# Prompt attention in a decoder layer: transposes and scores in one gap between weight tiles, scaling and softmax in the other

## The chip, the cores and the metric

The kernel runs on one core of one Trainium2 chip. The metric is device time in microseconds (us), the median of the runs shown. The engines are called as the profile calls them: PE (TensorE matmuls), PEld (its weight loads), DVE (VectorE), ACT (ScalarE), POOL (GpSimd) and SP (SyncE).

## The reference, cut to what matters

One layer of a hybrid decoder runs on a prompt of 256 rows and on 8 samples of 8 rows that share the weights. One input projection gives the columns of a short gated convolution (B, C, h), of attention (q, k, v) and of two gates. The change concerns only the prompt's attention: 16 query heads and 4 key heads of width 64, in blocks of 128 queries over at most 256 keys.

```
def window_attend(q, k, v, dist, valid, rel_bias, sinks):
    s = einsum(q, k) * HEAD_DIM ** -0.5
    s = where(valid, s + bias, -inf)
    m = maximum(max(s), sink)
    p = exp(s - m)
    p = p / (sum(p) + exp(sink - m))
    return einsum(p, v)
```

The rest of the layer is matrix products: the projections, two output projections, their gated sum through `w_o`, and a SwiGLU of width 5632.

## The kernel before, in words

All products go through `product`. Weights arrive in tiles of 4 x 128 rows by 256 columns (`wraw`, 4 buffers, loaded on SP's queue). ACT rounds each tile to a high part (`whi`, L129) and DVE takes the remainder (`wlo`, L130), three buffers each. PE then does 24 matmuls for a tile (L186): high by high, high by low, low by high, for 4 row chunks and 2 column blocks, each streaming 320 columns of activations. The first use of `wlo` is the ninth matmul of its tile.

Attention is side work. It is a Python generator, and `tick()` advances it by one `yield` after each weight tile of the products for q, C, H and B. What the generator emits between two yields therefore stands between two weight tiles in PE's order; a scheduler may move single instructions by a few places, and the order on each engine is then fixed. One gap between two weight tiles is called a gap here, and the work emitted into it a slot.

The prompt's attention has 8 units (a key head and a pair of query heads). For each unit i the functions are:

- `bias_load`: a DMA on POOL's queue that fetches the unit's bias (2 buffers, `bias`).
- `prompt_scores`: six score matmuls (L541 into `ps1`, L544 into `ps0`), then four DVE operations (L549 to L553) that add the bias and fold two parts into the tile `s` (3 buffers).
- `prompt_softmax`: a maximum on DVE (L561), two small DVE operations (L562, L566), four exponentials on ACT (L569) and a small one (L572).
- `prompt_norm`: denominator and reciprocal (L576, L577) and four scalings of `s` on DVE (L579).
- `prompt_pt`: four PE transposes of `s` (L585, into `pp`), a copy on ACT (L586) and two masked copies on DVE (L588) into `pT` (4 buffers).
- `prompt_pv`: for each pair of units, 12 products with v (L601, into `po`); both halves of `po` leave through ACT (L611, high part) and DVE (L612, low part). It runs for units 0 to 3 in step 6 and for units 4 to 7 in step 10.

`pp`, `ps1`, `ps0` and `po` all come from one ring of 4 PSUM buffers (`ps_aux`); a new one waits until the buffer's last content, four allocations earlier, has been read by DVE and ACT.

In step i the kernel before puts into one slot the scaling of unit i-2 (emitted at the end of the step ahead) and the scores of unit i; into the next slot the softmax of unit i, then any products with v, then the transposes of unit i-2.

Two places outside attention matter as well. After the prompt's attention come the samples' (L658 to L726), which puts a few more small groups of matmuls between weight tiles until about 221 us. From there on PE runs weight tile after weight tile; the next foreign matmuls are a sum over partitions (L207) at 715 us and a single short matmul of the function `nudge` (L914) at 729 us.

Of the kernel before, what the change touches and what calls it, by code (L numbers as in the profile page):

```python
# [52 lines left out]
def hybrid_layer(ctx: ExitStack, tc: tile.TileContext, a: dict, o: list):  # L53
# [18 lines left out]
    def ps_aux(name):  # L72
        return aux[0].tile([P, 512], F32, tag="aux", name=name)
# [3 lines left out]
    def u(s):  # L77
        uid[0] += 1
        return f"{s}_{uid[0]}"
# [129 lines left out]
    def flip(ap):  # L209

        *rest, (step, n) = ap.ap
        return bass.AP(ap.tensor, ap.offset + (n - 1) * step, [*rest, (-step, n)])
# [270 lines left out]
    def q2(ch, par):  # L483
        o = LEAD_A + ch * at_row + par * TP
        return at_t[:, o:o + TP]
# [34 lines left out]
    def bias_load(kv, gp):  # L520
        bias = pr.tile([P, 2, 2 * WIN], F32, tag="bias", name=u("bias"), bufs=2)
        nc.gpsimd.dma_start(
            bias,
            bass.AP(
                e_scr.tensor, e_scr.offset + (kv * GRP + gp * 2) * EL, [[1, P], [EL, 2], [1, 2 * WIN]]
            ),
        )
        return bias

    def prompt_scores(kv, gp, bias):  # L530

        j, par = kv // 2, kv % 2
        s = pr.tile([P, 4, WIN], F32, tag="s", name=u("s"), bufs=3)
        ps1, ps0 = ps_aux(u("ps1")), ps_aux(u("ps0"))
        for gi in range(2):
            q = q2(j * 4 + gp * 2 + gi, par)
            for i in range(2):  # L540
                nc.tensor.matmul(  # L541
                    ps1[:, gi * 256:(gi + 1) * 256], q[:, WIN:2 * WIN], k2[:, kv, i], start=i == 0, stop=i == 1
                )
            nc.tensor.matmul(  # L544
                ps0[:, gi * 256:(gi + 1) * 256].rearrange("p (two k) -> p two k", two=2), q[:, 0:WIN],
                k2[:, kv, :, 0:WIN], start=True, stop=True,
            )
        w = pr.tile([P, 2, 2 * WIN], F32, tag="w", name=u("w"), bufs=1)
        nc.vector.tensor_add(w, ps1.rearrange("p (g k) -> p g k", g=2), flip(bias))  # L549
        nc.vector.tensor_max(s[:, 2:4], w[:, :, 0:WIN], w[:, :, WIN:2 * WIN])  # L550
        p0 = ps0.rearrange("p (g two k) -> p g two k", g=2, two=2)
        nc.vector.tensor_add(s[:, 0:2], p0[:, :, 0], flip(bias[:, :, 0:WIN]))
        nc.vector.tensor_add(s[:, 0:2], p0[:, :, 1], s[:, 0:2])  # L553
        return s

    def prompt_softmax(kv, gp, s):
        h0 = kv * GRP + gp * 2
        mx = wk.tile([P, 2, 2], F32, tag="mx", name=u("mx"))
        den = wk.tile([P, 2, 2], F32, tag="den", name=u("den"))
        es = wk.tile([P, 2, 2], F32, tag="es", name=u("es"))  # L560
        nc.vector.tensor_reduce(mx.rearrange("p b g -> p (b g)"), s, axis=AX.X, op=ALU.max)  # L561
        nc.vector.scalar_tensor_tensor(  # L562
            mx, mx, -1.0, nsink[:, h0:h0 + 2].unsqueeze(1).to_broadcast([P, 2, 2]),
            op0=ALU.mult, op1=ALU.min,
        )
        nc.vector.tensor_add(es, sink_bc[:, h0:h0 + 2].unsqueeze(1).to_broadcast([P, 2, 2]), mx)  # L566
        for n in range(4):
            b, g = n // 2, n % 2
            nc.scalar.activation(  # L569
                s[:, n], s[:, n], AF.Exp, bias=mx[:, b, g:g + 1], accum_out=den[:, b, g:g + 1]  # L570
            )
        nc.scalar.activation(es, es, AF.Exp)  # L572
        return den, es

    def prompt_norm(s, den, es):
        nc.vector.tensor_add(den, den, es)  # L576
        nc.vector.reciprocal(den, den)  # L577
        for n in range(4):
            nc.vector.tensor_scalar(s[:, n], s[:, n], den[:, n // 2, n % 2:n % 2 + 1], None, op0=ALU.mult)  # L579

    def prompt_pt(s):
        pt = pr.tile([P, 3, 2 * WIN], F32, tag="pT", name=u("pT"), bufs=4)
        pp = ps_aux(u("pp"))
        for n in range(4):
            nc.tensor.transpose(pp[:, n * WIN:(n + 1) * WIN], s[:, n], ident)  # L585
        nc.scalar.activation(pt[:, 0, :], pp[:, 0:256], AF.Copy)  # L586
        for b in range(2):
            nc.vector.tensor_mul(  # L588
                pt[:, 1 + b, :].rearrange("p (g q) -> p g q", g=2),
                pp[:, 256:512].rearrange("p (g q) -> p g q", g=2),  # L590
                sides[:, b:b + 1].to_broadcast([P, 2, WIN]),
            )
        return pt

    def prompt_pv(j, gp, pts):
        po = ps_aux(u("po"))
        steps = ((0, 0, 0, True, True), (1, 0, 1, True, False), (1, 1, 2, False, True))
        for b, t, kb, st_, sp_ in steps:
            for par in range(2):
                kv = j * 2 + par  # L600
                nc.tensor.matmul(  # L601
                    po[par * 64:(par + 1) * 64, b * 256:(b + 1) * 256],
                    vn[t][:, kv * HD:(kv + 1) * HD], pts[par][:, kb, :], start=st_, stop=sp_,
                )
        for g in range(2):
            src = po.rearrange("p (b g s j) -> p g b s j", b=2, g=2, j=JS)[:, g]
            ch = j * 4 + gp * 2 + g
            two_to(*(x(ch)[:, 0:TP // JS, :].rearrange("p (b s) j -> p b s j", b=2) for x in (at_h, at_l)), src)
# [5 lines left out]
    def prompt_attention():  # L614
        units = [(j * 2 + par, gp) for j in range(2) for gp in range(2) for par in range(2)]
        bias, sc, sm, pts = {}, {}, {}, {}
        bias[0] = bias_load(*units[0])
        for i in range(len(units) + 3):
            if i < len(units):
                if i + 1 < len(units):  # L620
                    bias[i + 1] = bias_load(*units[i + 1])
                sc[i] = prompt_scores(*units[i], bias.pop(i))
                yield
                sm[i] = prompt_softmax(*units[i], sc[i])
            if i >= 3 and (i - 3) % 4 == 3:
                for n in (i - 5, i - 3):
                    kv, gp = units[n]
                    prompt_pv(kv // 2, gp, (pts.pop(n - 1), pts.pop(n)))
            if 0 <= i - 2 < len(units):
                pts[i - 2] = prompt_pt(sc.pop(i - 2))  # L630
            yield
            if 0 <= i - 1 < len(units):
                prompt_norm(sc[i - 1], *sm.pop(i - 1))
            if i >= len(units):
                yield

    W2 = WIN + TS

# [117 lines left out]
    def attention():  # L756
        yield from prompt_attention()
        pr_p.close()
        with tc.tile_pool(name="sm", bufs=1, side="right") as sm:
            yield from sample_attention(sm)  # L760
# [505 lines left out]
```

## Time and profile before

| what | value |
|---|---|
| median of 3 runs | 1601.17 us (1601.07 to 1602.27) |
| the profiled execution: its own time, its span | 1601.14 us, 1599.4 us |
| busy: PE, DVE, ACT | 1590.5, 885.7, 651.4 us |
| the prompt's attention (first score matmul to last product with v) | about 91 to 174 us |
| DVE busy from 120 to 140 us | 19.89 of 20 us |

The profile's span runs from the first to the last instruction; the time of the run is 1.7 us longer. The times of matmuls in the trace overlap: one matmul of 320 columns is shown with 302 ns, but the next one starts 140 ns later. So what a matmul costs PE is read from the distance of starts, or from the chain of work that ended last, whose pieces do not overlap.

### The profile page before, as it was taken

The numbers are of one execution on the slowest core, as the hardware profiler recorded it, in microseconds if no ns is written. First come the engines' busy times: TensorE is split into PE (matmuls) and PEld (weight loads), VectorE is DVE, ScalarE is ACT, GpSimd is POOL, SyncE is SP. The second block draws the span as 40 slices with busy tenths as digits, with TensorE's granted clock in tenths as the row PEclk, the third lists the DMA queues.
The fourth block names the chain that finished last, engine by engine and source line by source line (L and its number), as shares of the span: only waits on it lengthen the run. The fifth ranks groups of instructions, "written<-read, shape, count | busy, mean of one in ns | idle before, by whom it ended". The sixth has DMA issues, their size and how long they took to land.

```text
span 1599.4 us, 26405 instructions
## 1 busy us (share of the span) xinstructions
PE 1590.5 (99%) x10955; PEld 1555.2 (97%) x10955; DVE 885.7 (55%) x1315; ACT 651.4 (41%) x928; POOL 78.3 (5%) x123
## 2 busy tenths in 40 slices
PE   9999999999999999999999999999999999999998
PEld 9999999999999999999999999998888999999887
DVE  7879565445555555556555555553444455555556
ACT  7555433433333334444333333333333334444443
POOL 1101311000000003320000000000000000000000
PEclk9999999999999999999999999999999999999999
DMA  8554546545454544544444455455555544545552
GB/s 276 174 168 138 184 146 195 169 156 156 156 157 157 159 158 158 157 156 152 157 158 159 158 158 158 157 153 163 155 156 157 156 157 158 159 158 157 185 173 93
DMA packets 74399, 258.13 MB, mean 161 GB/s; under 512 B 8552, under 2 KB 11928, under 8 KB 74152
## 3 DMA queue, kind: packets, MB, share of 16 engines
q1 hardware_dynamic: 71880, 249.86, 49.6%
q0 software_dynamic: 1968, 5.90, 1.3%
q8 instruction: 86, 1.41, 0.4%
q10 hardware_dynamic: 432, 0.69, 0.1%
q14 instruction: 33, 0.27, 0.0%
HBM read 253.30 MB, written 5.08 MB: 162 GB/s over the span
## 4 chain that ended last, share of the span: by engine, by line
PE 99%; DVE 0%; ACT 0%; issue 0%; DVEq 0%
PE fu L186 19%; PE fg L186 18%; PE dn L962 9%; PE ga L186 7%; PE wo L186 7%; PE gc L186 7%; PE dn L970 6%; PE B L186 3%; PE C L186 3%; PE H L186 3%; PE ya L186 3%; PE yc L186 3%; PE q L186 3%; PE dl L966 2%; PE kv L366 2%; PE dn L1116 1%
## 5 line engine op out<-in xcount | busy, mean ns | idle before, releaser
L130 DVE TENSOR_TENSOR wlo<-wraw,whi 128x1024 fp32r<-128x1024 f32 (+1 forms) x461 | 562.5, 1220 | 584.7 <-ACT whi L129 473.2
L129 ACT ACTIVATE whi<-wraw 128x1024 fp32r<-128x1024 f32 (+1 forms) x461 | 485.8, 1055 | 713.0 <-PE fu L186 129.5
L186 PE MATMUL fu<-hl_t,whi 128*128 128x320 f32 x704 | 205.3, 302 | 0.0
L186 PE MATMUL fu<-hh_t,whi 128*128 128x320 f32 x704 | 205.3, 302 | 0.0
L186 PE MATMUL fg<-hh_t,whi 128*128 128x320 f32 x704 | 205.2, 302 | 0.0
L186 PE MATMUL fg<-hl_t,whi 128*128 128x320 f32 x704 | 205.2, 302 | 0.0
L186 PE MATMUL fu<-hh_t,wlo 128*128 128x320 f32 x704 | 159.0, 302 | 0.0
L186 PE MATMUL fg<-hh_t,wlo 128*128 128x320 f32 x704 | 158.9, 301 | 0.0
L962 PE MATMUL dn<-a_t,whi 128*128 128x512 f32 x640 | 157.9, 383 | 0.0
L186 PEld LDWEIGHTS fu<-hh_t,whi 128*128 128x128 f32 x704 | 131.9, 187 | 0.0
L186 PEld LDWEIGHTS fg<-hh_t,whi 128*128 128x128 f32 x704 | 131.8, 187 | 0.0
L186 PEld LDWEIGHTS fg<-hl_t,whi 128*128 128x128 f32 x704 | 131.8, 187 | 0.0
L186 PEld LDWEIGHTS fu<-hl_t,whi 128*128 128x128 f32 x704 | 131.8, 187 | 0.0
L962 PEld LDWEIGHTS dn<-a_t,whi 128*128 128x128 f32 x640 | 115.1, 188 | 15.0
L186 PEld LDWEIGHTS fu<-hh_t,wlo 128*128 128x128 f32 x704 | 116.3, 187 | 0.0
L186 PEld LDWEIGHTS fg<-hh_t,wlo 128*128 128x128 f32 x704 | 116.3, 187 | 0.0
L970 PEld LDWEIGHTS dn<-a_t,wlo 128*128 128x128 f32 x640 | 99.1, 188 | 7.9
L970 PE MATMUL dn<-a_t,wlo 128*128 128x320 f32 x640 | 105.8, 302 | 0.0
L186 PE MATMUL wo<-m_h,whi 128*128 128x320 f32 x256 | 74.6, 302 | 0.0
L186 PE MATMUL gc<-xh_t,whi 128*128 128x320 f32 x256 | 74.6, 302 | 0.0
L186 PE MATMUL ga<-xh_t,whi 128*128 128x320 f32 x256 | 74.6, 302 | 0.0
L186 PE MATMUL wo<-m_l,whi 128*128 128x320 f32 x256 | 74.6, 301 | 0.0
(308 smaller groups left out, 2655.2 us busy)
## 6 DMA issues: line engine op xcount, KB each, us to landing
wraw<-in_w_in_dram SPq DMA_DIRECT2D x128, 512.0 KB, 3.8
wraw<-in_w_gate_dram SPq DMA_DIRECT2D x88, 512.0 KB, 3.8
wraw<-in_w_up_dram SPq DMA_DIRECT2D x88, 512.0 KB, 3.7
wraw<-in_w_down_dram SPq DMA_DIRECT2D x88, 512.0 KB, 3.7
wraw<-in_w_o_dram SPq DMA_DIRECT2D x32, 512.0 KB, 3.8
wraw<-in_w_conv_out_dram SPq DMA_DIRECT2D x16, 512.0 KB, 3.7
wraw<-in_w_attn_out_dram SPq DMA_DIRECT2D x16, 512.0 KB, 3.7
wraw<-in_w_kv_dram SPq DMA_DIRECT2D x6, 512.0 KB, 6.9
```

The source lines that it names most:

```text
L129: last["hi"] = nc.scalar.activation(hi, src, AF.Copy)
L130: last["lo"] = nc.vector.tensor_sub(lo, src, hi.bitcast(F32))
L186: last["mm"] = nc.tensor.matmul(turns(fives(ps[c][:, :T])), w[:, k, c * P:(c + 1) * P], turns(x(kc)), start=(kc == 0 and i == 0), stop=(kc ...
L366: last["mm"] = nc.tensor.matmul(turns(fives(ps[c][:, :T])), w[:, k, c * P:(c + 1) * P], turns(x(kc)), start=(kc == 0 and m == 0), stop=(kc ...
L962: nc.tensor.matmul(turns(placed(ps[c])), parts[k][0][:, cs], turns(a_move(k)), start=k == 0, stop=False)
L966: nc.tensor.matmul(low, a_low(k), parts[k][0], start=k == 0, stop=k == nf - 1 and c0 < E0)
L970: last["mm"] = nc.tensor.matmul(turns(placed(ps[c])[:, :, 0:JT]), parts[k][1][:, cs], turns(a_move(k)[:, :, 0:JT]), start=False, stop=k == ...
L1116: nc.tensor.matmul(turns(placed(ps[c])[:, :, JR:]), held[k][0][:, cs], turns(a_move(k)[:, :, JR:]), start=k == 0, stop=k == nf - 1,)
```

## The change

The number and kind of all instructions stay the same. In step i, the slot ahead of the first yield now holds the products with v (if any), the transposes of unit i-2 and the scores of unit i; the slot behind it holds the scaling of unit i-1 and the softmax of unit i, with no PE work. So transposes and scaling of a unit come one weight tile earlier than before, and scores and softmax stay where they were. The diff:

```
         for i in range(len(units) + 3):
-            if i < len(units):
-                if i + 1 < len(units):
-                    bias[i + 1] = bias_load(*units[i + 1])
-                sc[i] = prompt_scores(*units[i], bias.pop(i))
-                yield
-                sm[i] = prompt_softmax(*units[i], sc[i])
             if i >= 3 and (i - 3) % 4 == 3:
                 for n in (i - 5, i - 3):
                     kv, gp = units[n]
                     prompt_pv(kv // 2, gp, (pts.pop(n - 1), pts.pop(n)))
             if 0 <= i - 2 < len(units):
                 pts[i - 2] = prompt_pt(sc.pop(i - 2))
+            if i < len(units):
+                if i + 1 < len(units):
+                    bias[i + 1] = bias_load(*units[i + 1])
+                sc[i] = prompt_scores(*units[i], bias.pop(i))
             yield
             if 0 <= i - 1 < len(units):
                 prompt_norm(sc[i - 1], *sm.pop(i - 1))
-            if i >= len(units):
-                yield
+            if i < len(units):
+                sm[i] = prompt_softmax(*units[i], sc[i])
+            yield
```

## The prediction

> **What bounds the kernel now.** I read the page's busy shares and clock first, then the chain that ended last, then PE's waits.
>
> ```profile
> span 1599.4 us, 26405 instructions
> PE 1590.5 (99%) x10955; PEld 1555.2 (97%) x10955; DVE 885.7 (55%) x1315; ACT 651.4 (41%) x928; POOL 78.3 (5%) x123
> PE 99%; DVE 0%; ACT 0%; issue 0%; DVEq 0%
> PE q L186 <- DVE wlo L130: 0.3, 1, 0.3
> ```
>
> The chain is PE for 99% of the span, and the last line is, beside one wait ahead of the first matmul, all that the waits of PE list. So the time is the sum of what PE does. The change adds and removes no instruction; it can move the time in three ways only: through what a gap between weight tiles costs PE, through a wait that it creates on PE, and through the pace at which PE runs the tiles in between. The chain in order of time gives the pieces of PE's work without overlap (start, length, what):
>
> ```profile
> 88.41 3.36 PE C L186 x24
> ...
> 107.45 3.38 PE H L186 x24
> 110.83 0.44 PE pp L585 x4
> 111.27 3.37 PE H L186 x24
> ...
> 130.42 0.23 PE ps L541 x2
> ...
> 138.31 0.23 PE ps L541 x2
> ...
> 139.03 3.38 PE C L186 x24
> 142.40 2.74 PE po L601 x24
> 145.14 0.59 PE pp L585 x4
> ```
>
> A weight tile takes 3.36 us when nothing stands ahead of it, 3.38 us behind scores and 3.37 us behind transposes. The six scores take 0.72 us (138.31 to 139.03), the four transposes 0.44 us, the products with v 2.74 us. The reader is to see that a gap costs what its own matmuls take and about 0.01 to 0.02 us more.
>
> **Part 1: fewer gaps.** Before, the prompt's attention opens 17 gaps: 8 with scores, 8 with transposes (one of them with products with v), one with products alone. Afterwards, by the built order, it opens 11, since the transposes of units 0 to 5 stand directly ahead of the scores of units 2 to 7. Six gaps less at 0.01 to 0.02 us are 0.1 us gained. The trace of before has no transposes followed by scores; the nearest rows are the two kinds of gap, so the bounds are 0 and 0.12 us, and I take 0.1.
>
> **Part 2: new waits on PE.** Transposes wait for the scaling of `s` on DVE, and both now come one weight tile earlier. The tightest of the eight is unit 3: before, its scaling ended at 129.15 us (row below), and its transposes now stand where the scores of unit 5 began, at 130.42. That leaves 1.3 us, and in the new order this scaling has no more work ahead of it than it had. I count 0; without that cover the cost is the lag itself.
>
> The PSUM ring of four is the second place. Every slot takes at most three buffers, except in step 6, where `po`, `po`, `pp`, `ps1` and `ps0` want five. So `ps0` takes the buffer of the first `po` in the same slot and must wait until ACT and DVE have taken out both halves of it. The built order shows it: the scheduler moved the two `ps0` matmuls behind three matmuls of the next tile. PE gets there at 138.31 + 2.74 + 0.59 + 2 x 0.23 + 3 x 0.14 = 142.52. When is the buffer free? DVE sets that, for it is full here:
>
> ```profile
> 120.00:140.00 20.00, 20.00 (x150) 19.99 (x148) 19.89 (x54) 12.15 (x38) 4.22 (x11) 1.00 0.51 161
> 128.68 0.47 DVE L579 TENSOR_SCALAR s<-s,den 128x128 f32<-128x128 f32 x2
> 139.37 0.69 DVE L549 TENSOR_TENSOR w<-ps,bias 128x512 f32<-128x512 f32 x1
> ...
> 140.97 0.28 DVE L579 TENSOR_SCALAR s<-s,den 128x128 f32<-128x128 f32 x1
> 141.16 0.68 DVE L561 TENSOR_REDUCE mx<-s 128x4 f32<-128x512 f32 x1
> 141.76 1.22 DVE L130 TENSOR_TENSOR wlo<-wraw,whi 128x1024 fp32r<-128x1024 f32 x1
> 142.89 0.16 DVE L562 SCALAR_TENSOR_TENSOR mx<-mx,nsink 128x4 f32<-128x4 f32 x1
> 173.48 0.42 DVE L612 TENSOR_TENSOR at_t<-po,at_t 128x256 fp32r<-128x256 f32 x1
> 174.35 0.87 DVE L612 TENSOR_TENSOR at_t<-po,at_t 128x256 fp32r<-128x256 f32 x2 [0.45 <-ACT at_t L611]
> ```
>
> (The first row is the busy table for 120 to 140 us; its fourth value is DVE: 19.89 of 20 us.) In the new order the evictions of `po` stand right behind the `wlo` split that in the old one ends at 142.89. The scores' adds (139.37 to 140.97, 1.60 us) and the maximum (141.16 to 141.76, 0.60 us) stood ahead of that split and now stand behind the evictions. So DVE gets to the first eviction between 142.89 - 2.20 = 140.69, if it uses all of that, and 142.89, if it waits for ACT instead. From the first DVE eviction to the end of the one that completes the first `po` it takes 173.48 to 174.35 + 0.42 = 174.77, that is 1.29 us. The buffer is free between 141.98 and 144.18, and PE loses between 0 and 1.66 us. I take the middle, 143.1, so 0.5 us: DVE loses some of the 2.2 us to earlier masked copies and to the exponentials that it waits for. What is queued behind the waiting `ps0` on PE is the rest of the weight tile and all tiles after it. The Trainium skill (TensorE: Matmul & The Clock Gate, Part 3) says that matmuls start and end in program order and only weight loads are pulled ahead, by which none of it can pass; no run here shows such a wait yet.
>
> Third, the weight split itself. DVE's queue is in a new order, so a `wlo` can come late. The smallest margin that I find between the end of a split and its first use, the ninth matmul of its tile, is at this row's:
>
> ```profile
> 103.48 1.22 DVE L130 TENSOR_TENSOR wlo<-wraw,whi 128x1024 fp32r<-128x1024 f32 x1
> 121.94 0.75 DVE L588 TENSOR_TENSOR pT<-pp,sides 128x256 f32<-128x256 f32 x2
> ```
>
> It ends at 104.70, and its tile begins at 107.45, so it is first used at 107.45 + 8 x 0.14 = 108.57: 3.9 us later. Within a pair of tiles DVE does the same work as before, and what is moved ahead of a split are the two masked copies of 0.75 us in sum. I count 0. DMAs: the order on SP's and on POOL's queue stays as it was; the bias of the next unit is released by the same DVE operation as before, which moves by less than these copies.
>
> **Part 3: the pace of the tiles.** This is the one thing in the trace that is worth more than a microsecond:
>
> ```profile
> 92.47 6.83 PE C L186 x48
> ...
> 153.62 3.42 PE H L186 x24
> ...
> 157.47 6.83 PE H L186 x48
> ...
> 193.32 7.03 PE C L186 x48
> 200.34 10.24 PE H L186 x72
> ...
> 240.00:700.00 460.00, 460.00 (x3287) 1.00 0.51 162
> 221.00:729.00 508.00, 507.63 (x3623) 1.00 0.50 160
> ```
>
> (The last two rows are the busy table of L186 on PE in two stretches.) From 240 to 700 us a matmul starts every 460 / 3287 = 139.95 ns. In the tiles above it is 10.24 / 72 = 142.2 ns. Each slow stretch begins at a gap and lasts to the next one. In all 288 matmuls are slow between these first and last rows, at 2.3 ns each 0.65 us. Which gap leaves the slow pace behind doesn't follow from its kind: of the eight gaps with scores, the first does and seven don't. From about 91 to 221 us, 5 of 20 gaps do. Afterwards there are fewer gaps but longer stretches, so I expect about the same sum: 0, with bounds of -0.65 us (all slow stretches gone) and about +1 us (most of 111 to 171 us slow: 17 tiles at 24 x 2.3 ns). The Trainium skill (TensorE: Matmul & The Clock Gate, Back-to-back issue gap) gives one distance for isolated warm matmuls, columns / 2.4 + 2.5 ns, which is 135.8 ns for 320 columns. By that rule a stream has one pace and this part and the first rival below are worth nothing; the trace shows two paces, both longer, so the rows decide.
>
> **Sum.** -0.1 + 0.5 + 0 = +0.4 us on the profiled execution's 1601.14 us (span 1599.4 and 1.7 around it), which stands 0.03 us below the median of 1601.17. Forecast 1601.6 us. Of its own this case reaches from 1601.17 - 0.65 - 0.12 = 1600.4 to 1601.17 + 1.66 + 1 = 1603.8 or so. A measurement of this kernel can tell about 0.2%, 3.2 us, from no change; so this is no change.
>
> **Rivals.**
>
> *Slower: the long stretch falls into the slow pace.* From the last gap at 221 us to the lone short matmul at 729 us nothing interrupts PE, and those 3623 matmuls are now fast. If the last gap of attention leaves the slow pace behind, every one costs 2.3 ns more: 8.2 us, 1609.8 us. For it speaks that no slow stretch in the trace ended without a gap, and that equal gaps came out both ways, so the outcome hangs on something finer than the order, which everything ahead shifts. Against it: that last gap consists of the same instructions as before, which came out fast. Five in 20 is the rate; I give 0.25. It decides at one gap, all or nothing.
>
> *Slower: DVE falls behind.* DVE is full from 120 to 140 us. If the 0.75 us of masked copies ahead of the adds are not caught up in any of the six joined slots, the lag is 4.5 us and passes the margin of 3.9 us from which PE begins to wait; with the margin gone beforehand, PE loses the whole 4.5 us, 1606.1 us. Against it: the same work leaves the other slot. 0.09.
>
> *Faster by over 0.2%.* All slow stretches and all six gaps gone give 1600.4 us, which is still no change. Nothing in PE's sum holds 3.2 us that this change could free; 0.06 for what I haven't seen.
>
> That the change doesn't do what it says falls away: the built order has the transposes directly ahead of the scores in six gaps.
>
> **Chances.** Forecast 0.60, slow pace 0.25, DVE behind 0.09, faster 0.06. So faster 0.06, same 0.60, slower 0.34. The range must reach to the slow pace, since without it 0.34 would be left out: 1600.4 (the forecast's lower bound) to 1610.4 (1609.8 and the 0.6 us by which the forecast's other terms can be worse).
>
> **What would show it.** Part 1: pieces of 0.44 us of transposes directly followed by 0.72 us of scores, and tiles of 3.36 to 3.38 us on both sides. Part 2: among the waits of PE and its weight loads a single new one of 0 to 1.7 us at L544, its releaser L612 on DVE, and none at L585 or for `wlo`. Part 3: x3623 between 221 and 729 us at 139.95 ns; at 142.2 ns the first rival is right. Several waits of PE for `wlo` between 110 and 150 us would be the second. A faster kernel with none of these would show that I misread what gaps cost.

## The result and the profile after

| | median (lowest to highest), runs |
|---|---|
| before | 1601.67 us (1600.89 to 1602.34), 22 |
| after | 1614.62 us (1601.83 to 1616.87), 22 |
| ratio after / before | 1.0051, 95% interval 1.0036 to 1.0067 |

The median hides the shape, and the ratio, which is near that of the means, does too (the medians alone would give 1.0081). The 22 runs of the kernel before lie in one group. Those of the changed kernel lie in two, with nothing between: 10 runs from 1601.83 to 1603.24 us (median 1602.36) and 12 from 1614.56 to 1616.87 us (median 1616.18). With 12 of 22 in the one, two runs more or less decide which group holds the median. They are called the lower and the upper group below; all three profiles that were taken of the changed kernel fell in the upper one. The lower group lies near the forecast of 1601.6 us, though without a profile of it nothing shows that it does so for the forecast's reasons. In the upper group the first rival ("the long stretch falls into the slow pace") came true, at a higher price than given: the median of all runs stands 4.2 us above the end of the range.

The page of the changed kernel, its span and busy times:

```profile
span 1612.9 us, 26406 instructions
PE 1603.3 (99%) x10955; PEld 1567.4 (97%) x10955; DVE 888.2 (55%) x1315; ACT 652.0 (40%) x928; POOL 78.5 (5%) x123
```

PE has as many instructions as before and is busy for 12.8 us longer; nearly all of the 13.5 us of span is therefore PE at work, not PE waiting. All that the waits of PE list (total us, times, longest):

```profile
PE wm L305 <- PEq L1248: 0.8, 1, 0.8
PE ps L544 <- DVE at_t L612: 0.7, 1, 0.7
PE q L186 <- DVE wlo L130: 0.3, 1, 0.3
```

One wait is new, the one at L544. The chain in order of time (start, length, what) shows the joined gaps and that wait:

```profile
107.64 6.72 PE H L186 x48
114.36 0.44 PE pp L585 x4
114.80 0.24 PE ps L541 x2
115.03 0.12 PE ps L544
115.15 0.23 PE ps L541 x2
115.39 0.12 PE ps L544
115.51 3.36 PE H L186 x24
...
142.36 0.43 DVE at_t L612
142.80 0.14 issue
142.93 0.47 PE ps L544 x2
```

Transposes (0.44 us) and scores (0.71 us together) now stand directly behind each other, and a pair of weight tiles takes 6.72 us, twice 3.36. Up to the last gap of attention, all this moves the time little. From there on the chain of the kernel before reads:

```profile
221.30 3.71 PE B L186 x25
...
701.99 13.44 PE fg L186 x96
715.73 13.66 PE fu L186 x96
729.46 13.49 PE fg L186 x96
...
1078.95 1.76 PE dn L962 x8
```

and that of the changed kernel:

```profile
221.68 3.33 PE B L186 x22
...
709.98 13.65 PE fg L186 x96
723.95 13.44 PE fu L186 x96
737.45 13.71 PE fg L186 x96
...
1092.49 1.78 PE dn L961 x8
```

The reader subtracts the starts of equal pieces. At the last gap the changed kernel is 0.38 us late (221.68 - 221.30), at `fg` 7.99 us, behind `nudge` still 7.99 us, at `dn` 13.54 us. So the loss comes in two stretches: 7.61 us from 222 to 710 us and 5.55 us from 737 to 1092 us. Between them both kernels change pace twice, at the sum over partitions (L207, ahead of `fu`) and at `nudge` (behind it), in opposite directions: before, the 96 matmuls of `fg`, `fu`, `fg` take 13.44, 13.66, 13.49 us, afterwards 13.65, 13.44, 13.71. The busy table of L186 in two stretches, first before, then after, says the same by counts:

```profile
740.00:1070.00 330.00, 330.00 (x2360) 1.00 0.50 157
```

```profile
240.00:700.00 460.00, 460.00 (x3236) 1.00 0.50 159
740.00:1070.00 330.00, 330.00 (x2322) 1.00 0.49 155
```

Against 139.95 ns per matmul before, it is now 460 / 3236 = 142.15 ns from 240 to 700 us, and from 740 to 1070 us 142.12 ns against 139.83. PE's granted clock is 1.00 in all of these rows, and PE is busy without a break: the same matmuls simply start 2.2 to 2.3 ns further apart.

The paces part earlier than the times do. Around the products with v at 172 us, first before, then after:

```profile
168.15 3.42 PE B L186 x24
171.57 2.74 PE po L601 x24
...
184.61 6.72 PE C L186 x48
```

```profile
168.58 3.36 PE B L186 x24
171.94 2.74 PE po L601 x24
...
185.12 6.83 PE C L186 x48
...
193.94 6.94 PE C L186 x48
200.88 10.09 PE H L186 x72
```

Before, the tile ahead of these products is slow (3.42 us) and the pace behind them fast (6.72 us for 48 matmuls); afterwards the tile is fast (3.36) and the pace behind slow (6.83). At the next gap (L657) both turn over again: 6.94 and 10.09 us here, against 7.03 and 10.24 in the prediction's lines. Ten kept profiles have this gap undivided and every tile at its address, and they agree: the five with the order of before go from slow to fast there, the five with joined gaps from fast to slow. So the two orders differ in pace ahead of 172 us already. Just ahead of the last gap both kernels are fast (3.36 us for the tile) and yet leave it differently: the pace that is seen isn't all that is carried.

### The profile page after: what moved, and what is told of

Same layout as the page of the kernel before. It is cut to its first block, busy times and chain, and to the rows that moved or that the text cites. A ratio compares the mean times of both kernels' runs of the same rounds, so it can differ in the third digit from the quotient of the medians.

```text
span 1612.9 us, 26406 instructions
## 1 busy us (share of the span) xinstructions
PE 1603.3 (99%) x10955; PEld 1567.4 (97%) x10955; DVE 888.2 (55%) x1315; ACT 652.0 (40%) x928; POOL 78.5 (5%) x123
## 4 chain that ended last, share of the span: by engine, by line
PE 98%; DVE 1%; issue 0%; ACT 0%; DVEq 0%
PE fg L186 19%; PE fu L186 19%; PE dn L961 9%; PE ga L186 7%; PE wo L186 7%; PE gc L186 7%; PE dn L969 6%; PE ya L186 3%; PE yc L186 3%; PE H L186 3%; PE B L186 3%; PE C L186 3%; PE q L186 3%; PE dl L965 2%; PE kv L366 2%; PE dn L1115 1%
## 5 line engine op out<-in xcount | busy, mean ns | idle before, releaser
L186 PE MATMUL fg<-hl_t,whi 128*128 128x320 f32 x704 | 206.9, 303 | 0.0
L186 PE MATMUL fu<-hl_t,whi 128*128 128x320 f32 x704 | 206.7, 303 | 0.0
L186 PE MATMUL fg<-hh_t,whi 128*128 128x320 f32 x704 | 206.5, 303 | 0.0
L186 PE MATMUL fu<-hh_t,whi 128*128 128x320 f32 x704 | 206.3, 302 | 0.0
L186 PE MATMUL fg<-hh_t,wlo 128*128 128x320 f32 x704 | 159.7, 302 | 0.0
L186 PE MATMUL fu<-hh_t,wlo 128*128 128x320 f32 x704 | 159.6, 302 | 0.0
L186 PEld LDWEIGHTS fg<-hh_t,whi 128*128 128x128 f32 x704 | 131.7, 187 | 0.0
L186 PEld LDWEIGHTS fg<-hl_t,whi 128*128 128x128 f32 x704 | 131.7, 187 | 0.0
L186 PEld LDWEIGHTS fu<-hh_t,whi 128*128 128x128 f32 x704 | 131.7, 187 | 0.0
L186 PEld LDWEIGHTS fu<-hl_t,whi 128*128 128x128 f32 x704 | 131.7, 187 | 0.0
L186 PEld LDWEIGHTS fg<-hh_t,wlo 128*128 128x128 f32 x704 | 116.6, 187 | 0.0
L186 PEld LDWEIGHTS fu<-hh_t,wlo 128*128 128x128 f32 x704 | 116.6, 187 | 0.0
L186 PE MATMUL ga<-xl_t,whi 128*128 128x320 f32 x256 | 75.6, 304 | 0.0
L186 PE MATMUL gc<-xl_t,whi 128*128 128x320 f32 x256 | 75.6, 304 | 0.0
L186 PE MATMUL wo<-m_l,whi 128*128 128x320 f32 x256 | 75.6, 304 | 0.0
L186 PE MATMUL gc<-xh_t,whi 128*128 128x320 f32 x256 | 75.3, 303 | 0.0
```

Of the source, the lines that this page charges most:

```text
L186: last["mm"] = nc.tensor.matmul(turns(fives(ps[c][:, :T])), w[:, k, c * P:(c + 1) * P], turns(x(kc)), start=(kc == 0 and i == 0), stop=(kc ...
```

## The experiments

What had to be told apart: **theory A**, the timing: the new wait for DVE leaves PE's stream a little different from run to run, so that the pace behind the later gaps is a matter of the run. **Theory B**, the order: it is the joined gaps alone that leave the pace open or slow. All experiments are compared with runs of the kernel before on the same chip.

**The wait taken away, by two more gaps.** In the changed kernel, the products with v of the second pair of units go to the other slot of the step, so that step 6 never wants five buffers:

```
-                for n in (i - 5, i - 3):
-                    kv, gp = units[n]
-                    prompt_pv(kv // 2, gp, (pts.pop(n - 1), pts.pop(n)))
+                n = i - 5
+                kv, gp = units[n]
+                prompt_pv(kv // 2, gp, (pts.pop(n - 1), pts.pop(n)))
...
+            if i >= 3 and (i - 3) % 4 == 3:
+                n = i - 3
+                kv, gp = units[n]
+                prompt_pv(kv // 2, gp, (pts.pop(n - 1), pts.pop(n)))
```

> The changed kernel, with one edit: the products with v of the second pair of units move to the other slot, so the joined slot of step 6 wants four PSUM buffers and not five, and PE no longer waits for the eviction of po; transposes and scores stay joined. Theory A (timing): that wait, which ends when DVE is done and not at a fixed place in PE's own sequence, shifts PE by an amount that differs from run to run, and so the pace that the last gap leaves behind differs too. Expected by A: all runs in one group, most likely 1601 to 1602 us (one group near 1610 or 1615 us would fit A too), no wait of PE at L544. Theory B (order): the joined gaps alone put PE into the slow pace; expected by B: two groups again, near 1602 and near 1615 us, wait or no wait.

Measured: 1602.41 us (1601.41 to 1603.52, 11 runs, one group), ratio 1.0004 (0.9995 to 1.0013). The waits of PE no longer list L544, and from 240 to 700 us x3288 are counted, the fast pace. The chain around the products with v at 172 us, which this edit divides too:

```profile
168.48 3.36 PE B L186 x24
171.84 1.45 PE po L601 x12
173.29 3.61 PE B L186 x24
176.90 1.45 PE po L601 x12
178.34 6.92 PE B L186 x48
```

The wait is gone, transposes and scores are still joined, and all 11 runs are in the lower group. That is what A expects, but two gaps have been added (13 instead of 11), and the trace shows one of them at work. In the tile between the two halves of the products the starts are 142.1 ns apart ((176.17 - 173.47) / 19), behind the second half 140.0 ((181.74 - 178.52) / 23): the first half turns the fast pace into the slow one, as the undivided products do in the changed kernel's profiles, and the second turns it back. So the added gap can account for the lower group by itself, and the run says nothing for A.

**The wait put into the kernel before, first try, with its control.** A 4-column matmul waits for a copy on DVE behind the scores of unit 6; in the control it reads a constant instead and waits for nothing. The next weight tile's matmuls are ordered behind it. The copy has a small tile of its own; in the control, `ones.to_broadcast([P, 4])` stands in place of `s[:, 2, 0:4]`:

```
+    def dve_mark(s):
+        g = wk.tile([P, 4], F32R, tag="gm", name=u("gm"), bufs=1)
+        nc.vector.tensor_copy(g, s[:, 2, 0:4])
+        mark["gm"] = nc.tensor.matmul(ps_aux(u("gm"))[:, :4], ones_r, g, start=True, stop=True)
...
+                if i == 6:
+                    dve_mark(sc[i])
```

> The kernel before, with a wait put in: behind the scores of unit 6 stands a matmul of 4 columns that reads 4 columns which DVE copies from the finished scores, and the next weight tile is held behind it. PE waits there some 2 us for DVE. Gaps and their order are those of before. Theory A (timing): two groups of runs, one near 1603 to 1604 us and one 8 to 13 us above. Theory B (order): one group near 1603 to 1604 us.

> Control of the kernel with the wait put in: the same matmul of 4 columns at the same place, but it reads 4 columns that DVE has copied some 7 us earlier from a constant, so PE does not wait. Theory A (timing): one group, 1601.2 to 1602 us if the extra matmul does not change the pace that later gaps leave; one group 8 to 13 us above if it does. Theory B (order): one group near 1601.5 us.

Measured: 1643.28 us (1640.87 to 1643.75, 4 runs; ratio 1.0256, 1.0242 to 1.0270) with the wait, and 1639.11 us (1638.49 to 1640.03, 4 runs; ratio 1.0234, 1.0220 to 1.0248) without it. The control shows that the test failed as a test of the wait: something else costs about 38 us (1639.11 - 1601.46 of the kernel before on that chip). Its profile runs slow from the start, long before unit 6: two weight tiles for q at 33 us take 6.93 us, in the kernel before 6.72 at 32 us. The suspect was the tile of 16 bytes, which moves every later tile in SBUF.

**The small tile alone.** The kernel before, with a tile that nothing reads:

```
+    pad = wk.tile([P, 4], F32, tag="gm", name="pad", bufs=1)
+    nc.gpsimd.memset(pad, 0.0)
```

> The kernel before with one unused tile of 16 bytes per partition ahead of all later tiles in SBUF, set once on GpSimd; no instruction on TensorE, VectorE or ScalarE differs, and there is no wait. If it was the shift of addresses that made the two kernels with the small gm tile slow: 1636 to 1641 us, with matmuls of 320 columns near 142 to 144 ns nearly everywhere. If it was their extra matmul and copy: 1601 to 1603 us.

Measured: 1640.20 us (1639.99 to 1640.42, 2 runs), ratio 1.0238 (1.0220 to 1.0257). Its chain holds, among others:

```profile
610.83 109.23 PE wo L189 x768
720.05 13.87 PE fg L189 x96
```

The 768 matmuls of `wo` run at 142.2 ns (109.23 / 768), but the tiles of `fg` at 144.4 to 144.5 (13.87 / 96), a third pace, slower than both others, and it stays so behind L207 and `nudge`. The mean from 240 to 700 us, over both, is 460 / 3197 = 143.9 ns. PE's instructions are the same and no wait is new. Beside the shift of addresses the edit adds one memset on POOL at the start; the control above has no such memset and counts x3197 in that stretch too. So the pace depends on where tiles lie in SBUF (which operands moved isn't seen in the traces), and both runs above say nothing of the wait.

**The wait in the kernel before, no tile moved.** The same edit with the copy in a buffer of an existing small tile (`tag="mx"`), and its control:

> The kernel before with a wait put in, as in the first such kernel, but the 4 columns that DVE copies lie in a buffer that exists already, so that no other tile changes its place in SBUF (in the first attempt a new small tile moved everything behind it, and every stage ran at the slow pace). PE waits some 2 us for DVE at the scores of unit 6. Theory A (timing): runs in two groups, near 1603.5 us and 8 to 14 us above. Theory B (order): one group near 1603.5 us.

> Control: the same extra matmul of 4 columns at the same place, on 4 columns that DVE has copied long before, so PE does not wait. Theory A (timing): one group (1601.5 us, or 8 to 14 us above if the extra matmul turns the pace). Theory B (order): one group near 1601.5 us.

Measured: 1605.69 us (1604.38 to 1607.00, 8 runs; ratio 1.0023, 1.0013 to 1.0033) with the wait, 1601.85 us (1601.02 to 1602.76, 11 runs; ratio 0.9999, 0.9990 to 1.0008) without. The wait that it made:

```profile
PE gm L619 <- DVE gm L618: 2.3, 1, 2.3
```

A wait three times as long as the changed kernel's, at about the same time, leaves one group, and the long stretch at the fast pace (x3288 from 240 to 700 us, as in the control). It costs 3.8 us over the control, 1.5 us more than the wait. The two profiles are 3.4 us apart, and 0.9 of it stands ahead of attention (the first tile for C begins at 88.90 us against 88.01); beyond that the difference wasn't followed. Theory A in its bare form, that a wait on DVE is enough, falls. This control differs from the one with the small tile in one line, the buffer of the 4 columns, which bears out what the small tile alone showed: 1601.85 us instead of 1639.11, on two chips on which the kernel before differs by 0.5.

**One short matmul behind the last gap of the kernel before.** It asks whether the pace of the long stretch hangs on a single small thing. `nudge0` is `nudge` with rows of `xh` and `xl` as operands:

```
+    def nudge0(n):
...
+        nc.tensor.matmul(ps_aux(u("nudge"))[:, :n], w, x, start=True, stop=True)
...
+        yield
+        nudge0(P)
         yield
```

> The kernel before, with one more matmul of 128 columns, alone between two weight tiles just behind the last gap of attention, at about 228 us. It costs about 0.1 us by itself. If a gap turns one pace into the other (as the sum over partitions at 715 us and the lone matmul at 729 us did in the two traces: fast to slow and slow to fast), all runs are slow from there to the sum over partitions: 1601.7 + 3570 x 2.3 ns = about 1609.9 us or more. If a lone matmul always leaves the fast pace behind: 1601.8 us. If the outcome is drawn anew in each run: two groups.

Measured: 1615.24 us (1614.16 to 1615.46, all 4 runs), ratio 1.0083 (1.0069 to 1.0096). The chain around it, and the busy table of L186:

```profile
222.05 6.93 PE B L186 x48
228.98 0.06 PE nudge L616
229.04 3.05 PE B L186 x21
```

```profile
240.00:700.00 460.00, 460.00 (x3237) 1.00 0.51 159
740.00:1070.00 330.00, 330.00 (x2323) 1.00 0.49 155
```

One instruction of 0.06 us on the chain costs 13.8 us (1615.24 - 1601.46 of the kernel before on that chip), and the profile is that of the upper group in both stretches. The gap at L207 and the matmul of `nudge` each turn the pace over, so a slow first stretch brings the fast 96 matmuls and the slow second stretch with it.

**Two such matmuls, one weight tile apart.**

```
+        yield
+        nudge0(P)
+        yield
+        nudge0(P)
         yield
```

> The kernel before with two lone matmuls of 128 columns behind the last gap of attention, one weight tile apart (one of them made it 1615.2 us in all runs). If a lone matmul turns fast into slow and slow into fast: the slow pace lasts one weight tile only, 1601.9 us. If it always leaves the slow pace behind: 1615 us again.

Measured: 1602.00 us (1601.38 to 1603.00, 10 runs), ratio 1.0000 (0.9991 to 1.0009). The chain:

```profile
228.53 0.06 PE nudge L616
228.59 3.48 PE B L186 x24
232.07 0.06 PE nudge L616
232.13 7.89 PE C L186 x56
```

The weight tile between the two takes 3.48 us, slow; behind the second, 56 matmuls take 7.89 us, 140.9 ns each with the first after the gap among them, and from 240 to 700 us x3288 are counted again. The second matmul undoes what the first does, in all 10 runs.

**The changed kernel again, twice.** A profile of the lower group was wanted, and the share of the groups.

> The changed kernel once more, for one more profile of it. Both theories: about 1602.3 us with 139.95 ns from matmul to matmul between 222 and 715 us, or about 1615 to 1616.5 us with 142.2 ns there; the pieces up to 143 us, with the wait at L544, the same in both.

> The changed kernel again, unaltered, beside the one without its wait. Both theories: runs in two groups, 1602 to 1603 and 1614.5 to 1617 us, each with a third or more of them. The profile is at 142.2 ns per matmul between 222 and 722 us where its run is in the upper group, at 139.95 ns where it is in the lower one; a profile of the lower group would show from which gap on the two part.

Measured: 1615.21 us in the single run, and 8 runs of 1602.70, 1602.77, 1603.37 and five from 1614.53 to 1616.19 us (ratio 1.0051, 1.0025 to 1.0077). Both profiles were of the upper group, with the wait of 0.7 us at L544. In all, 13 of 31 runs of the changed kernel are in the lower group. What a lower run looks like was not seen. The three profiles of the upper group don't begin alike: from 88 to 108 us the last one has the other pace (its first tile for C takes 3.41 us and the next two 6.72, in the other two 3.36 and 6.83). From 109 us on, ahead of the wait, all three agree. So this early difference doesn't decide the group.

**The wait taken away, all gaps kept.** For the first pair of units the low part of `po` is set to zero on POOL, so that only ACT reads that PSUM buffer. Left out is that low part alone.

```
     def two_to(dh, dl, src, low=True):
         nc.scalar.activation(dh, src, AF.Copy)
+        if not low:
+            nc.gpsimd.memset(dl.bitcast(F32), 0.0)
+            return
         nc.vector.tensor_sub(dl, src, dh.bitcast(F32))
...
-                    prompt_pv(kv // 2, gp, (pts.pop(n - 1), pts.pop(n)))
+                    prompt_pv(kv // 2, gp, (pts.pop(n - 1), pts.pop(n)), low=n != 1)
```

> The changed kernel with its one new wait taken away and its gaps kept: for the first pair of units (step 6) the low part of the products with v isn't taken on VectorE but set to zero on GpSimd, so the PSUM buffer that ps0 (L544) wants is read by ScalarE alone and free before TensorE gets there. Left out: that low part, for one of four pairs. The order on TensorE differs from the changed kernel's by three matmuls: the two of ps0 stand with those of ps1 instead of three weight-tile matmuls later. Theory A2 (the wait, whose end is set by VectorE and so differs a little from run to run, makes the pace behind the later gaps a matter of the run): no wait at L544, and all runs in one group, 1601.5 to 1603 us, or all near 1615 us. Theory B (the joined gaps alone leave the pace open): no wait at L544 and still two groups about 13 us apart, the upper in a third or more of the runs.

> The same kernel as in the run without the wait in the changed kernel (joined gaps kept; low part of the products with v of the first pair of units left out), once more, since five runs in the upper group could be chance: the changed kernel itself came out in the lower group in 13 of 31 runs. Theory A2 (the run-dependent part comes through the wait): again all runs at 1613 to 1616.5 us. Theory B (the gaps alone leave it open): each run has about 4 chances in 10 to be at 1601 to 1603 us, so some of them are there.

Measured: 1614.41 us (1613.41 to 1615.84, 5 runs; ratio 1.0078, 1.0065 to 1.0090), then 1615.02 us (1614.07 to 1615.60, 5 runs; ratio 1.0084, 1.0070 to 1.0098). The chain of the first, at the place of the former wait:

```profile
144.19 0.12 PE ps L544
144.31 6.74 PE C L186 x48
```

No wait, x3236 from 240 to 700 us in both profiles, and 10 of 10 runs in the upper group. At the changed kernel's share of 18 upper runs in 31, ten in a row would have a chance of 0.4%. So the order needs no wait for the slow pace: the joined gaps without it cost the 13 us in every run, which is B's part. For A there remains only that the lower runs (4 in 10) came with the wait and not without it. That the wait makes the split is not shown, since besides it two more things differ here: the two `ps0` matmuls stand three matmuls earlier than in the changed kernel, and DVE has two operations less (POOL sets the zeros).

The two profiles of this one kernel hold a warning. In the first the pairs of weight tiles between joined gaps are slow, in the second fast, from the same instructions:

```profile
109.48 6.84 PE H L186 x48
```

```profile
108.20 6.72 PE H L186 x48
```

Yet behind the products with v of step 6 (140.27 and 138.55 us) both are fast, and from there on they have the same pace everywhere. So a difference between runs is there up to the place of the former wait, and in this kernel the gap there wipes it out. Whether in the changed kernel the wait brings in a difference of its own or lets an earlier one through stays open; one lone short matmul behind the changed kernel's last gap, which should make its upper runs fast, wasn't tried either.

## Why the prediction was right or wrong

**Part 1, fewer gaps (right, and small).** Pieces of 0.44 and 0.71 us with weight tiles of 3.36 us on both sides, as described; a joined gap costs no more than its own matmuls. The bounds were a little short: nine tiles, four scores and four transposes take 34.93 us before (103.38 to 138.31) and 34.79 afterwards (103.13 to 137.92), so 0.14 us for four gaps less, where 0.12 was the most for six.

**Part 2, the new wait (right).** Its place (L544), its releaser (L612) and its being the only one were as told. PE lost 0.7 us where 0.5 was taken (0 to 1.66). The buffer came free at 142.79 (forecast 143.1), and PE could have gone on at 142.06, one matmul behind the one shown at 141.92 in the timeline, not 142.52. No wait of PE at L585, none for `wlo`: the second rival, DVE falling behind, didn't happen. But the tightest transposes weren't those of unit 3 with 1.3 us: in step 6 the scaling of unit 4 ended at 140.45 us (139.58 + 0.87), 0.2 us before its transposes began at 140.66.

```profile
141.50 1.29 DVE L612 TENSOR_TENSOR at_t<-po,at_t 128x256 fp32r<-128x256 f32 x3
141.92 0.31 PE L186 MATMUL C<-xh_t,whi 128*128 128x320 f32 x1
```

The sum of all steps up to the last gap was forecast at +0.4 us and is +0.38 us in the chain. That this fits so well is luck: the changed kernel's profile begins attention 0.26 us early (88.15 us against 88.41, the first tile for C), and from there to the last gap it takes 0.64 us longer (133.53 against 132.89). The lower group stands 0.69 us above the runs before.

**Part 3, the pace (the step that failed).** "About the same sum" of slow stretches was expected, and against the first rival that the last gap "consists of the same instructions as before, which came out fast". The same instructions came out slow in the upper runs, 18 of 31 (in all three that were profiled). The pace behind a gap hangs on the gap and on the state in which the stream arrives: one matmul of 0.06 us turns it over, and the next one back. Counting slow gaps as a rate (5 in 20, hence 0.25) treated as independent draws what is carried along: the kernel before came out fast in all its runs, and the joined gaps without the wait slow in all ten. Nor does it "decide at one gap": the profiles of the two kernels are opposite around the products with v at 172 us already, 50 us ahead of the last gap.

**The price (mis-sized).** The term of 8.2 us was about right for its stretch (7.61 us up to 710 us); it is 3623 x 2.25 ns (142.2 - 139.95), with the 2.3 ns as printed it would be 8.3. What was missing is the rest: L207 and `nudge` turn the pace over as well, so that the stretch from 737 to 1092 us becomes slow with the first, another 5.55 us. The forecast's own profile had the sign of it: before, 96 matmuls of `fu` took 13.66 us between two stretches at the fast pace. With both stretches the rival would have read 0.4 + 7.6 + 5.6 = 13.6 us, 1614.7, and the range would have reached there. This is the profiled run's 1614.67; the upper group's median of 1616.18 lies higher. Of such spread the three profiles show the place: their runs of 1614.67, 1615.21 and 1615.88 us begin the first tile for C at 88.15, 88.85 and 89.32, so nearly all of it arises ahead of attention.

The Trainium skill (TensorE: Matmul & The Clock Gate, Back-to-back issue gap) gives, for isolated warm matmuls, one distance for a number of columns, by its formula 135.8 ns for 320. No run here agrees: distances of 139.9, 142.1 and 144.4 ns were measured for matmuls of 320 columns in a stream at a granted clock of 1.00. The Trainium skill (the same page, Part 3) also says that matmuls start and end in program order. This case's trace agrees: the matmul that stood behind the waiting `ps0` began at 143.24 us, behind the two `ps0` that began at 142.93.

## What to carry to other kernels

Where PE is the bound and thousands of equal matmuls follow one small gap, look at the distance of their starts in the busy table by stage, not only at waits: here 2.2 ns per matmul outweighed everything that the change did by design. Before a change to the order of small work is judged, put one lone short matmul, then two, behind the last gap: in the kernel before, one cost 13.8 us and two 0.1 (in the changed kernel it wasn't tried). Where such a jump is as large as the difference between two kernels, look for the pace first. Take many runs, since a median of two groups says little, and keep every tile at its address when an experiment adds one.

## What was unexpected of the hardware

- PE's stream of 320-column matmuls keeps one of at least three paces (139.9, 142.1, 144.4 ns) over hundreds of microseconds, and a single short matmul changes it (13.8 us for one, 0.1 us for two).
- The 24 products with v at 172 us turn the pace over in ten profiles of ten, in both directions; divided into 12 and 12 with a weight tile between them, they turn it over and back.
- An unused tile of 16 bytes per partition, allocated ahead of later tiles in SBUF, made the kernel before 38.3 us slower (1640.20 against 1601.89 us).
- The pace can differ between two runs of one kernel at the same place (6.84 against 6.72 us for two weight tiles) and agree again behind a later gap. What in PE or its operand reads carries the pace isn't shown by these traces.
